# Dense products of a two-block transformer kernel: one float32 matmul each in place of three passes over split operands

## The chip, the cores and the metric

The kernel runs on one core of one Trainium2 chip, and the metric is the device time of one execution in microseconds. The engines are named as the profile names them: PE (TensorE's matmuls), PEld (its weight loads), DVE (VectorE), ACT (ScalarE), POOL (GpSimd), SP (the queue that issues most DMAs). TensorE's clock has two levels, 1.2 and 2.4 GHz; the profile gives the granted share of the higher one.

## The reference, cut to what matters

Two blocks follow each other, all in float32 (512 tokens, 1024 features). The first mixes tokens with a gated recurrence and a windowed attention, then sends the tokens through 16 experts. The second runs two layers over 16 + 512 tokens.

```python
# first block
h = rms_norm(x, norm1_g) * (1 + scale1) + shift1
proj = h @ w_in
mix = jnp.concatenate([y_mlstm, y_attn], axis=-1) @ w_out
x = x + gate1 * mix
x = x + gate2 * expert_choice_ffn(h2, ...)      # 16 experts of 64 tokens each
# second block, each of two layers (D = 1024, D_FF = 2816)
proj = h @ w_in
h = layer_norm(ALPHA * h + mix @ w_out, ln1_g, ln1_b)
y = (silu(h @ w1) * (h @ w3)) @ w2
h = layer_norm(ALPHA * h + y, ln2_g, ln2_b)
```

The products by `w_in`, `w_out`, `w1`, `w3` and `w2` outside the experts are the dense products of this document.

## The kernel before, in words

Features lie on partitions and tokens along the free dimension, so a dense product multiplies 128 x 128 weights (stationary) with 512, 264 or 256 tokens (moving) and sums over 8 feature tiles, or over the tiles of a part of the hidden features, in a bank of PSUM. The value projections have it the other way: 128 tokens stationary, 256 columns of weights moving.

Each operand is split: `split_w` (L416) makes `hi`, a copy by ACT in the type float32r, and `lo`, the rest, by DVE. `split_x` (L429, L430) does the same for products of the kernel's own, and the norms write `hi` and `lo` of the layer input (L1461, L1462). A product is then three matmuls on float32r operands: hi by hi, hi by lo, lo by hi (`mmh`, L1377 to L1379; `mmk`, L1389 to L1391, the same for several weight tiles; `values`, L717 to L719 and L1618 to L1620; `block`, L1985 to L1987).

The rest of PE's work has plain float32 operands: the experts (up L1171, down L1195, transposes L1182, gather L1154, scatter L1266), the sum of squares of the first norm (L570, eight matmuls), the attention and the recurrence, the rotation of the retention heads (L1588, one matmul for each of 4 tiles, 2 halves of the tokens and 2 layers).

The order of the work is written by a small planner, `_Stream`. Dense products stand in jobs. A job loads its weights some jobs ahead (`deep`), splits them some microseconds of announced cost ahead (`lead`), and its run yields the cost that it announces for each product, `3 * n / 2400.0` for n columns. Between the units of attention and recurrence, which go through generators, `S.step(STEP1)` or `S.step(STEP3 / 2)` emits so much announced cost of dense products. So the numbers set how many products stand between two units; the engines run in the order in which things were emitted.

Weights come in pieces of 1 MB through a ring, of 4 places in the first block and 2 in the second; a place is free when its weights are split. The input of the first dense product needs the results of `ada` jobs, which load two pieces each (L536) and multiply them at L555.

The upward products of the feed-forward, from the fourth tile of hidden features on, use Winograd's form of Strassen's product (`seven`): seven block products of 4 matmul products each, with sums of weights by DVE (L2004, L2005) and POOL (L2010, L2011), and sums of the layer input (`sums`) by POOL and DVE. `out` multiplies the two results and splits them into `H`; `down` multiplies `H` by `w2`, and `resid` (L1397, L1399) adds into `h`.

The layer input stands in `h` (for the residual) and split in `X`. During the mixer of the second block the values take the place of `h`, and when the last feature tile of the mixer is there, POOL adds `X`'s two parts back into `h` (L1911, 16 instructions a layer).

Of the kernel before, what the change touches and what calls it, by code (L numbers as in the profile page):

```python
# [12 lines left out]
F32R = mybir.dt.float32r  # L13
# [43 lines left out]
def _packed(v):  # L57
    """Features of the four retention heads in three tiles: a head of the first three each, and a third of the last."""
# [41 lines left out]
def _host(inp):  # L100
# [88 lines left out]
    # tables that depend on shapes alone  # L189
# [45 lines left out]
# ---------------------------------------------------------------- the program  # L235
# [9 lines left out]
class _Job:  # L245
# [11 lines left out]
    def prep(self, whole=True):  # L257
        """the rest of the preparation, or one step of it"""
# [12 lines left out]
class _Stream:  # L271
    """Dense products in the order of their emission. A job is prepared in two steps, the load of its weights
    (for the next `deep` jobs) and their split (`lead` us ahead). Its run yields the tensor engine's time in us, or None
    while it cannot go on; what has to wait for another engine goes to a tail."""
# [5 lines left out]
    def add(self, key, prep, run, cost=5.0, slow=0):  # L280
        """slow: the time between the steps of a preparation that goes along with the jobs before it"""
# [23 lines left out]
    def tail(self, g, job=None):  # L305
        """goes on with the steps of g, each after as much time as the one before it yields"""
# [16 lines left out]
    def _one(self):  # L323
        """emits one piece, returns its cost in us"""
# [30 lines left out]
    def until(self, key, flush=False):  # L355
        """goes on until the job is done; flush: its tails at once"""
# [13 lines left out]
    def weave(self, g, first, us):  # L370
        """the rest of the jobs, a step of g after each `us`"""
# [7 lines left out]
def _pipe(units):  # L379
    """the stages of the units, one behind the other"""  # L380
# [12 lines left out]
class _K:  # L393
    def __init__(self, nc, tc, A, at, out, dbg=None):
        self.nc, self.tc, self.A, self.at, self.out = nc, tc, A, at, out
        self.dbg = dbg or {}
        self.pin = False
# [905 lines left out]
    def second(self, ctx):  # L1303
# [17 lines left out]
        for c, g in self.cache.items():  # L1321
# [4 lines left out]
            if c == 0:  # L1326
                _drain(ln[0])
# [808 lines left out]
```

## Time and profile before

| what | before |
| --- | --- |
| device time, median of 3 runs | 2675.08 us (2674.12 to 2677.49) |
| profiled execution, span | 2671.3 us (the profile gives no other time for it) |
| PE, PEld busy | 2561.6, 1822.5 us |
| DVE, ACT, POOL busy | 1308.1, 849.1, 370.0 us |
| matmul records | 16400 |
| HBM read | 566.19 MB, 213 GB/s over the span |

The span is the time from the first to the last instruction of the profiled execution; its busy times are sums over the whole span, which has three parts: the mixer of the first block (to about 390 us), the experts (to about 1343), the second block. Records of matmuls overlap in time, since matmuls are pipelined.

### The profile page before, as it was taken

To read this page: it belongs to the slowest core of one execution; us is meant where nothing else is said; L and a number is where in the kernel's file an instruction comes from. 1 tells how busy PE (TensorE), PEld (TensorE's weight loads), DVE (VectorE), ACT (ScalarE), POOL (GpSimd) and SP (SyncE) were. 2 spreads that over 40 slices of the span, in tenths; PEclk is the share of its full clock that TensorE was granted. 3 is DMA by queue.
4 is the path that set the end of the run, shared out by engine and by line. 5 is a ranking of instruction groups with operands and counts; after the bars stand their busy time and mean duration, and the time that the engine had idled before them with its cause. 6 is when DMAs were issued, how large, how long until landed. Compare 5 with 4: busy or idle time off the path is not lost.

```text
span 2671.3 us, 39752 instructions
## 1 busy us (share of the span) xinstructions
PE 2561.6 (96%) x16400; PEld 1822.5 (68%) x16400; DVE 1308.1 (49%) x2483; ACT 849.1 (32%) x1601; POOL 370.0 (14%) x361
## 2 busy tenths in 40 slices
PE   7999989999999999999989998999999999899997
PEld 4777765333343433333478878999999888899997
DVE  5476750101010110101273568878876447978796
ACT  3455541000001010000133435434443434534344
POOL 0000010000000000000040125112223013511123
PEclk9999989999999999999989999999999999999999
DMA  7522459999999999999922112223332211232332
GB/s 306 192 93 96 166 196 384 420 402 419 419 419 420 420 420 419 420 419 419 379 86 90 45 57 81 93 95 102 105 109 94 88 46 56 95 103 88 102 108 73
DMA packets 104673, 570.93 MB, mean 214 GB/s; under 512 B 11598, under 2 KB 14926, under 8 KB 50988
## 3 DMA queue, kind: packets, MB, share of 16 engines
q1 hardware_dynamic: 101148, 561.45, 53.4%
q10 hardware_dynamic: 3344, 6.94, 0.8%
q8 instruction: 129, 2.11, 0.3%
q14 instruction: 52, 0.43, 0.0%
HBM read 566.19 MB, written 2.16 MB: 213 GB/s over the span
## 4 chain that ended last, share of the span: by engine, by line
PE 82%; DVE 12%; ACT 2%; DMA 2%; issue 1%; POOL 1%; DVEq 0%; ACTq 0%; POOLq 0%
PE gu L1171 18%; PE py L1195 8%; PE d L1377 6%; PE d L1379 6%; PE d L1378 6%; PE s L1985 5%; PE s L1987 5%; PE s L1986 5%; PE sc L1266 3%; PE sc L1154 3%; DVE wlo L416 2%; PE gt L1182 1%; DVE qlo L1462 1%; DMA ring<-in_w 1%; PE d L1618 1%; PE d L1619 1%
## 5 line engine op out<-in xcount | busy, mean ns | idle before, releaser
L416 DVE TENSOR_TENSOR wlo<-ring,whi 128x1024 fp32r<-128x1024 f32 (+2 forms) x253 | 305.3, 1210 | 126.2 <-ACT whi L416 125.7
L416 ACT ACTIVATE whi<-ring 128x1024 fp32r<-128x1024 f32 (+2 forms) x253 | 248.7, 989 | 354.3 <-PE d L1378 130.7
L1186 DVE TENSOR_TENSOR hd<-sg,gt 128x256 f32<-128x256 f32 x64 | 27.0, 422 | 640.9 <-ACT sg L1184 640.9
L1377 PE MATMUL d<-phi,whi 128*128 128x264 f32 (+1 forms) x888 | 254.4, 287 | 10.5 <-DVE h L1399 7.3
L1378 PE MATMUL d<-plo,whi 128*128 128x264 f32 (+1 forms) x888 | 251.0, 283 | 0.2
L1379 PE MATMUL d<-phi,wlo 128*128 128x264 f32 (+1 forms) x888 | 250.6, 282 | 0.0
L1171 PE MATMUL gu<-ew,xin 128*64 128x512 f32 x1008 | 247.8, 595 | 0.0
L1171 PE MATMUL gu<-ew,late 128*64 128x512 f32 x1024 | 247.4, 595 | 0.0
L1195 PE MATMUL py<-ew,hd 128*64 128x512 f32 x960 | 242.3, 599 | 0.0
L1173 ACT ACTIVATE gus<-gu 128x512 f32<-128x512 f32 x64 | 38.2, 597 | 486.5 <-PE gu L1171 486.5
L1171 PEld LDWEIGHTS gu<-ew,late 128*64 128x64 f32 x1024 | 75.2, 137 | 152.5 <-issue 148.2
L1377 PEld LDWEIGHTS d<-phi,whi 128*128 128x128 f32 x888 | 166.7, 188 | 17.8 <-issue 11.9
L1171 PEld LDWEIGHTS gu<-ew,xin 128*64 128x64 f32 x1008 | 81.7, 137 | 140.4 <-issue 128.6
L1378 PEld LDWEIGHTS d<-plo,whi 128*128 128x128 f32 x888 | 167.3, 188 | 1.4 <-DVE plo L430 0.6
L1379 PEld LDWEIGHTS d<-phi,wlo 128*128 128x128 f32 x888 | 167.2, 188 | 0.2 <-issue 0.2
L1377 PE MATMUL d<-qhi,whi 128*128 128x264 f32 (+1 forms) x496 | 151.9, 306 | 2.3 <-ACT qhi L1461 1.8
L1195 PEld LDWEIGHTS py<-ew,hd 128*64 128x64 f32 x960 | 69.9, 136 | 118.4 <-issue 112.4
L1378 PE MATMUL d<-qlo,whi 128*128 128x264 f32 (+1 forms) x496 | 146.8, 296 | 1.5 <-DVE qlo L1462 1.5
L1379 PE MATMUL d<-qhi,wlo 128*128 128x264 f32 (+1 forms) x496 | 146.8, 296 | 0.0
L1225 POOL TENSOR_TENSOR late<-h 128x528 f32<-128x528 f32 x1 | 1.3, 1315 | 946.7 <-ACT late L1223 946.7
L2010 POOL TENSOR_TENSOR ring<-ring 128x512 f32<-128x512 f32 x38 | 59.3, 1560 | 441.9 <-DVE glo L416 425.3
L1377 PEld LDWEIGHTS d<-qhi,whi 128*128 128x128 f32 x496 | 97.8, 197 | 14.1 <-issue 3.9
(492 smaller groups left out, 5950.4 us busy)
## 6 DMA issues: line engine op xcount, KB each, us to landing
ew<-in_wg SPq DMA_DIRECT2D x127, 1024.0 KB, 17.3
ew<-in_wu SPq DMA_DIRECT2D x127, 1024.0 KB, 16.1
ew<-in_wd SPq DMA_DIRECT2D x120, 1024.0 KB, 17.3
ring<-in_w SPq DMA_DIRECT2D x44, 1024.0 KB, 4.9
ring<-in_win SPq DMA_DIRECT2D x22, 1024.0 KB, 4.9
ring<-in_wada SPq DMA_DIRECT2D x21, 1024.0 KB, 6.2
ring<-in_wout SPq DMA_DIRECT2D x16, 1024.0 KB, 5.0
ring<-in_w SPq DMA_DIRECT2D x24, 640.0 KB, 3.9
```

The source lines that it names most:

```text
L416: both = (nc.scalar.activation(hi[:, :n], w, AF.Copy), nc.vector.tensor_sub(lo[:, :n], w, hi[:, :n].bitcast(F32)))
L1154: nc.tensor.matmul(ps[:, j], self.tok[:, t, 128 * k:128 * k + 128], oh[:, t].rearrange("p a b -> p (a b)"), start=(t == 0), stop=(t == 3))
L1171: nc.tensor.matmul(ps[64 * j:64 * j + 64], x, ws[k // 4][j][:, o], start=(k == 0), stop=(k == 7))
L1195: nc.tensor.matmul(py[64 * c:64 * c + 64], hd[:, j], wd[j // 2][:, o:o + 512], start=(n == 0 and j == 0), stop=(n == 3 and j == 3))
L1266: nc.tensor.matmul(ps, ys[e][s, 128 * (k % 4):128 * (k % 4) + 128], ogs[e][s], start=(i == 0), stop=(i == len(es) - 1))
L1377: nc.tensor.matmul(ps[:, :n], a, X[0][:p, k, r], start=(i == 0 and part != 1), stop=False)
L1378: nc.tensor.matmul(ps[:, :n], a, X[1][:p, k, r], start=False, stop=False)
L1379: nc.tensor.matmul(ps[:, :n], b, X[0][:p, k, r], start=False, stop=(i == len(ks) - 1 and part != 0))
L1985: nc.tensor.matmul(ps, a, x[0][:, k], start=(k == 0), stop=False)
L1986: nc.tensor.matmul(ps, a, x[1][:, k], start=False, stop=False)
L1987: nc.tensor.matmul(ps, b, x[0][:, k], start=False, stop=(k == 3))
L2010: nc.gpsimd.tensor_sub(a11, a21, a11)
```

## The change

Every dense product becomes one matmul on float32 operands, as they were loaded or computed. `split_w` and `split_x` go, with the tiles for the parts. The rings get 7 and 8 places, and a place is held until the last product with its weights. The layer input has a tile of its own (`X`, two buffers in the second block), the residual reads it from there, the norms write it once, and POOL's copies back go. The Winograd sums read `X` and write plain tiles. The announced costs and the steps all shrink to about two thirds. The comments of the file go as well.

```diff
-STEP1 = 4.0
-STEP3 = 2.4
+STEP1 = 2.7
+STEP3 = 1.6
...
-SUMGAP, PLAIN, HOLD, SLOW = 3.0, 3, 12.0, 2.1
+SUMGAP, PLAIN, HOLD, SLOW = 2.0, 3, 8.0, 2.0
...
-    def split_w(self, w, n, at=None):
-        hi, lo = [pool.tile([128, cols], F32R, name=tag + i, tag=tag + i, bufs=bufs) for i in ("hi", "lo")]
-        both = (nc.scalar.activation(hi[:, :n], w, AF.Copy), nc.vector.tensor_sub(lo[:, :n], w, hi[:, :n].bitcast(F32)))
...
-    def split_x(self, hi, lo, src):
-        nc.scalar.activation(hi, src, AF.Copy)
-        nc.vector.tensor_sub(lo, src, hi.bitcast(F32))
...
-        self.rp, self.ringcols, self.rbufs = pool("rp1"), 2048, 4
-        self.spl, self.nspl = pool("spl1"), 2
+        self.rp, self.ringcols, self.rbufs = pool("rp1"), 2048, 7
...
-                nc.scalar.activation(X[0][:, k], x, AF.Identity, scale=am[:, k:k + 1], bias=mod[:, k:k + 1])
-                nc.vector.tensor_scalar(x, x, am[:, k:k + 1], mod[:, k:k + 1], op0=OP.mult, op1=OP.add)
-                nc.vector.tensor_sub(X[1][:, k], x, X[0][:, k].bitcast(F32))
+                if k % 2:
+                    nc.scalar.activation(X[:, k], x, AF.Identity, scale=am[:, k:k + 1], bias=mod[:, k:k + 1])
+                else:
+                    nc.vector.tensor_scalar(X[:, k], x, am[:, k:k + 1], mod[:, k:k + 1], op0=OP.mult, op1=OP.add)
...
-                    ins = nc.tensor.matmul(ps, y_[0][s, o], og_[0][s], start=True, stop=False)
+                    ins = nc.tensor.matmul(ps, y[s, o], og[s], start=True, stop=True)
...
-                    nc.tensor.matmul(ps, y_[0][s, o], og_[1][s], start=False, stop=False)
-                    nc.tensor.matmul(ps, y_[1][s, o], og_[0][s], start=False, stop=True)
...
-        self.rp, self.ringcols, self.rbufs = pool("rp3"), 2048, 2
-        self.spl, self.nspl = pool("spl3"), 4
+        self.rp, self.ringcols, self.rbufs = pool("rp3"), 2048, 8
...
     def xt(self, n, k):
-        return tuple(self.xp.tile([128, k, L2], F32R, name=n + p, tag=n + p) for p in ("hi", "lo"))
+        return self.xp.tile([128, k, L2], F32, name=n, tag=n, bufs=2 if n == "q" else 1)
...
     def mmh(self, ps, r, ks, X, order=None, part=None, cut=None):
-            (hi, lo), j, k, p = ks[i if order is None else order[i]]
-            a, b = hi[:p, 128 * j:128 * j + 128], lo[:p, 128 * j:128 * j + 128]
-            nc.tensor.matmul(ps[:, :n], a, X[0][:p, k, r], start=(i == 0 and part != 1), stop=False)
-            nc.tensor.matmul(ps[:, :n], a, X[1][:p, k, r], start=False, stop=False)
-            nc.tensor.matmul(ps[:, :n], b, X[0][:p, k, r], start=False, stop=(i == len(ks) - 1 and part != 0))
-            yield 3 * n / 2400.0
+            w, j, k, p = ks[i if order is None else order[i]]
+            nc.tensor.matmul(ps[:, :n], w[:p, 128 * j:128 * j + 128], X[:p, k, r], start=(i == 0 and part != 1),
+                             stop=(i == len(ks) - 1 and part != 0))
+            yield 2 * n / 2400.0
...
-    def resid(self, m, r, ps, alpha):
+    def resid(self, m, r, ps, X=None):
...
-            self.nc.vector.scalar_tensor_tensor(x, x, alpha, ps, op0=OP.mult, op1=OP.add)
+            self.nc.vector.scalar_tensor_tensor(x, X[:, m, r], ALPHA, ps, op0=OP.mult, op1=OP.add)
...
-                hi, lo = X[0][:, k, r], X[1][:, k, r]
-                nc.scalar.activation(hi, t, AF.Identity, bias=bc)
-                nc.vector.scalar_tensor_tensor(lo, t, bc, hi.bitcast(F32), op0=OP.add, op1=OP.subtract)
-                if keep:
-                    nc.scalar.activation(x, t, AF.Identity, bias=bc)
+                nc.scalar.activation(X[:, k, r], t, AF.Identity, bias=bc)
...
-                for r in RO:
-                    for k in range(8):
-                        nc.gpsimd.tensor_add(self.h[:, k, r], X[0][:, k, r].bitcast(F32), X[1][:, k, r].bitcast(F32))
...
+                nc.gpsimd.tensor_sub(T[1][:, k], X[:, k, B_], X[:, k, A_])
+                nc.vector.tensor_sub(T[3][:, k], X[:, k + 4, B_], X[:, k, B_])
+                nc.gpsimd.tensor_sub(T[2][:, k], X[:, k + 4, B_], T[1][:, k])
+                nc.vector.tensor_sub(T[4][:, k], X[:, k + 4, A_], T[2][:, k])
...
-                nc.tensor.matmul(ps, a, x[0][:, k], start=(k == 0), stop=False)
-                nc.tensor.matmul(ps, a, x[1][:, k], start=False, stop=False)
-                nc.tensor.matmul(ps, b, x[0][:, k], start=False, stop=(k == 3))
-                yield 3 * nt / 2400.0
+                nc.tensor.matmul(ps, w[:, 128 * k:128 * k + 128], x[:, k], start=(k == 0), stop=(k == 3))
+                yield 2 * nt / 2400.0
...
-            nc.vector.tensor_mul(x, x, s[1][:, a:b])
-            self.split_x(H[0][:, place[f], r], H[1][:, place[f], r], x)
+            nc.vector.tensor_mul(H[:, place[f], r], x, s[1][:, a:b])
...
-                nc.gpsimd.tensor_sub(a11, a21, a11)
-                nc.gpsimd.tensor_sub(a12, a12, a11)
-                c = self.split_w(s3, 512, (fp, "c", 512, 2))
+                nc.gpsimd.tensor_sub(s2, a21, a11)
+                nc.gpsimd.tensor_sub(s4, a12, s2)
```

On PE, in the first Winograd tile of layer 0, the first block product ends and the second begins before with these rows (`qhi`, `qlo` the layer input, `t12` the sums of the input, `g` and `w` the split weights and their sums), one row for each pass:

```order
L1985 MATMUL s<-qhi,ghi 128x264
L1986 MATMUL s<-qlo,ghi 128x264
L1987 MATMUL s<-qhi,glo 128x264
L1985 MATMUL s<-t12hi,whi 128x264
L1986 MATMUL s<-t12lo,whi 128x264
L1987 MATMUL s<-t12hi,wlo 128x264
```

and now, from the second block product of that tile to its last (`t` the sums of the input, `ws` those of the weights, `ring` the weights as loaded):

```order
L1913 MATMUL s<-t_8350,ws 128x264 x4
L1913 MATMUL s<-q,ring 128x264 x4
L1913 MATMUL s<-t_8351,ws 128x264 x4
L1913 MATMUL s<-t_8349,ring 128x264 x4
L1913 MATMUL s<-t_8352,ring 128x264 x4
L1913 MATMUL s<-q,ws 128x264 x4
```

The 84 matmuls of a tile, three for a product, are 28, four in each row, and they read the ring itself.

On DVE, in the first norm of the second block (`var` its statistics, `nt` the normed input before the shift, `qlo` the low part of X, `wlo` that of weights), the second four feature tiles of the first half of the tokens stand before as

```order
L1459 SCALAR_TENSOR_TENSOR nt<-nt,cols,var 128x264 x4
L1462 SCALAR_TENSOR_TENSOR qlo<-nt,cols,qhi 128x264 x4
L1434 SCALAR_TENSOR_TENSOR var<-s,var 128x264
L416 TENSOR_TENSOR wlo<-ring,whi 128x1024 x2
L1435 TENSOR_SCALAR var<-var 128x264
L1583 TENSOR_SCALAR f<-d,cols 32x264
```

and the whole of that half now as

```order
L1216 SCALAR_TENSOR_TENSOR h<-sc,mod,h 128x512 x2
L1198 TENSOR_TENSOR late<-late,gus 128x528 x2
L1399 SCALAR_TENSOR_TENSOR var<-s,var 128x264
L1400 TENSOR_SCALAR var<-var 128x264
L1424 SCALAR_TENSOR_TENSOR nt<-nt,cols,var 128x264 x8
```

The eight multiplications of a half stand together, with no low part and no weight split among them.

## Rows read from the trace of the kernel before

**Rows 1.** Busy us of the engines by stretch (us from the start); records in brackets

```profile
core 0: us, PE busy (x) PEld busy (x) DVE busy (x) ACT busy (x) POOL busy (x), PEclk, DMA share, GB/s
0.00:390.00 390.00, 359.28 (x2205) 261.47 (x2206) 246.16 (x613) 192.36 (x403) 19.26 (x27) 0.97 0.46 175
390.00:1325.00 935.00, 920.50 (x4210) 363.06 (x4212) 96.80 (x163) 89.66 (x172) 0.00 (x0) 1.00 1.00 413
1343.00:1365.00 22.00, 16.25 (x58) 12.73 (x58) 19.87 (x30) 9.95 (x21) 13.36 (x15) 0.66 0.41 143
1700.00:2000.00 300.00, 297.30 (x2425) 295.43 (x2423) 238.57 (x365) 122.80 (x173) 62.51 (x46) 1.00 0.31 103
```

**Rows 2.** Line L1985, 1745 to 1756: count, ns min/median/max, first to last start

```profile
L1985 PE MATMUL s<-t12hi,whi x8: 280/284/287, 1746.0 to 1753.0; 128*128 128x264 f32 x8
L1985 PE MATMUL s<-qhi,whi x8: 280/284/287, 1747.5 to 1750.0; 128*128 128x264 f32 x8
L1985 PE MATMUL s<-qhi,ghi x8: 281/284/286, 1750.4 to 1754.4; 128*128 128x264 f32 x8
L1985 PE MATMUL s<-phi,chi x7: 281/283/291, 1744.9 to 1755.9; 128*128 128x264 f32 x7
```

**Rows 3.** Line L1377, 2448 to 2456: the same columns

```profile
L1377 PE MATMUL d<-phi,whi x24: 277/281/283, 2447.7 to 2455.9; 128*128 128x256 f32 x24
```

**Rows 4.** Timeline, PE, 512 columns: start us, duration us, line

```profile
48.87 0.39 PE L1377 MATMUL d<-xhi,whi 128*128 128x512 f32 x1
...
50.23 0.39 PE L1377 MATMUL d<-xhi,whi 128*128 128x512 f32 x1
```

**Rows 5.** Timeline, PE, around a rotation in layer 0 (L1588)

```profile
1390.10 1.94 PE L1588 MATMUL s<-rx,c_perm 128*128 128x264 f32 x8
1391.69 0.47 PE L1618 MATMUL d<-whi,qhi 128*128 128x256 f32 x1
1392.00 0.28 PE L1619 MATMUL d<-wlo,qhi 128*128 128x256 f32 x1
```

**Rows 6.** Groups by line and form: record count, busy us, mean ns of one

```profile
L1154 PE MATMUL sc<-oh,tok 128*128 128x128 f32 x512 | 71.4, 290 | 1.2 <-DVE oh L1146 1.2
...
L570 PE MATMUL o<-sq,ones 128*128 128x512 f32 x16 | 9.9, 787 | 7.2 <-ACT sq L569 7.2
```

**Rows 7.** Timeline, PE: gather with new weights each time, and heads (L796, L799)

```profile
1028.95 2.50 PE L1154 MATMUL sc<-oh,tok 128*128 128x128 f32 x20
...
136.42 1.12 PE L796 MATMUL s<-h,blk 128*128 128x512 f32 x2
137.38 1.02 PE L799 MATMUL s<-h,blk 128*128 128x512 f32 x2
```

**Rows 8.** Page, groups of instructions: busy us, mean ns, idle before

```profile
L416 DVE TENSOR_TENSOR wlo<-ring,whi 128x1024 fp32r<-128x1024 f32 (+2 forms) x253 | 305.3, 1210 | 126.2 <-ACT whi L416 125.7
L416 ACT ACTIVATE whi<-ring 128x1024 fp32r<-128x1024 f32 (+2 forms) x253 | 248.7, 989 | 354.3 <-PE d L1378 130.7
```

**Rows 9.** Timeline, DVE and POOL, first norm of the second block

```profile
1350.81 2.69 DVE L1462 SCALAR_TENSOR_TENSOR qlo<-nt,cols,qhi 128x264 fp32r<-128x264 f32 x4
...
1344.94 5.25 POOL L1458 TENSOR_TENSOR nt<-h,mu 128x264 f32<-128x264 f32 x6 [1.80 <-ACT mu L1432]
```

**Rows 10.** Waits of PE, 1343 to 2671: total us, times, longest us

```profile
PE d L1377 <- DVE h L1399: 7.3, 9, 1.4
PE d L1377 <- DVE h L1397: 5.6, 9, 2.1
...
PE s L1985 <- ACT fu L2022: 4.6, 2, 3.5
...
PE d L1389 <- DVE fs L2069: 2.0, 2, 1.2
```

**Rows 11.** Waits of SP's DMA queue, 0 to 60: total us, times, longest us

```profile
SPq L597 <- DVE wlo L416: 17.2, 2, 12.6
SPq L536 <- PE s L555: 12.9, 3, 6.2
```

More of the change, by code (lines that the diff above doesn't have):

```diff
@@ L706, in prep, with run @@
                 yield
-                return [self.split_w(w[:, 1024 * j:1024 * j + 1024], 1024) for j in range(2)]
-            def run(pcs):
+                return w
+            def run(w):
                 if "v" not in at:
@@ L948, in run @@
                 n = slice(rs[0].start, rs[-1].stop)
-                yield from self.mmh(ps, n, [(pc, k, k, 128) for k in range(8)], Y, order)
+                yield from self.mmh(ps, n, [(pc, k, k, 128) for k in range(8)], mix, order)
                 for r in rs:
@@ L1001, in first_mixer @@
         lb = scv[:, 64:80]
-        while active or (S.left() and Y is None):
+        while active or (S.left() and not out):
             for g in list(active):
@@ L1007, in first_mixer @@
             S.step(STEP1)
-            if not S.left() and Y is None:
-                Y = tuple(xp.tile([128, 8, 512], F32R, name="y" + p, tag="x" + p) for p in ("hi", "lo"))
+            if not S.left() and not out:
+                out = True
                 for c in range(4):
@@ L1200, in down_last @@
             s1, s2 = self.s12 = [hold()[1][:, L2 * i:L2 * i + L2] for i in range(2)]
-            parts = place(F32R)
-            og_, y_ = [[parts[:, 1024 * i + 512 * j:1024 * i + 512 * j + 512] for j in range(2)] for i in range(2)]
-            self.split_x(*og_, og)
+            y = place()[:, :512]
             def products(c, py, wd, js):
@@ L1421, with norm @@
     stats, seen = {}, {}
-    def norm(self, g, b, r, X, keep=True):
+    def norm(self, g, b, r, X):
         nc, h = self.nc, self.h
@@ L1471, in pair, with halves_of @@
         yield
-        return [self.split_w(w[:, n * j:n * j + n], n, at) for j in range(m)]
-    def halves_of(self, name, l, R, ws, n, run, cost, at={}, head=None):
+        return [w[:, n * j:n * j + n] for j in range(m)]
+    def halves_of(self, name, l, R, ws, n, run, cost, head=None):
         kept = {}
@@ L1490, in one @@
             job(c, r, lambda _: run(c, r, kept[c], js), cs, cost)
-        last = [c for c in range(4) if c in at or c > 1]
         if head:
@@ L1497, in halves_of, with wout @@
             one(c, R[0], (c,))
-        for c in (2, 3, 1, 0):
-            one(c, R[1], () if c in last else (c,))
-    def wout(self, l, R, M, order):
+        for c in range(4):
+            one(c, R[1], ())
+    def wout(self, l, R, M, order, X):
         def end(m, r, ps):
-            self.resid(m, r, ps, ALPHA)
+            self.resid(m, r, ps, X)
             self.stat(m, r)
@@ L1565, in run @@
                             between(m, r)
-            S.add(ms, prep, run, 5.4 * len(ms))
+            S.add(ms, prep, run, 3.6 * len(ms))
         qk = {}
@@ L1608, in prep, with run @@
                 yield
-                return [self.split_w(w[:, 1024 * j:1024 * j + 1024], 1024) for j in range(2)]
-            def run(pcs):
+                return w
+            def run(w):
                 for t in range(5):
@@ L1914, in step @@
                 out = True
-                self.wout(l, RO, M, order)
+                self.wout(l, RO, M, order, X)
                 S.prep()
-        while active or not out or not back:
+        while active or not out:
             for g in list(active):
@@ L2040, in run @@
                     self.lnexp()
-            S.add(("up", l, f), prep, run, 9.3, SLOW)
+            S.add(("up", l, f), prep, run, 6.2, SLOW)
         def up(fs):
```

176 lines of the change are left out of this document (61 added, 115 removed).

## The prediction, made before the change was run

> **What bounds the kernel now.** I read the busy time by stretch first, then the stream of matmuls in time, then the counts by form, and last the waits. [rows 1] shows three kinds of stretch. From 0 to 390 us the mixer of the first block keeps PE 359 us busy. From 390 to 1325 us the experts run with the DMA engines at a share of 1.00 and 413 GB/s: that stretch is paced by 1 MB transfers, and its products are float32 already. After it the second block is PE again: 297.3 of 300 us in the feed-forward of layer 0, at a granted clock of 1.00 and with DMA at 0.31. Only around 1343 to 1365, where the first norm of the second block stands, is PE at 16.3 of 22 with DVE at 19.9. So what an edit does to the dense products lands on the span in the first and third part and nowhere else.
>
> A busy PE says little of its pace, since the records overlap, so I take start to start. In [rows 2] 31 first passes of Winograd blocks with 264 tokens start within 11.0 us: 30 steps of 0.367 us, one step being a whole product of three passes. With 256 columns [rows 3] it is 23 steps in 8.2 us, 0.357. With 512 columns [rows 4] two products take 1.36 us, 0.68 each. Per pass that is 122, 119 and 227 ns: 0.42 ns for each further column, one column per cycle at 2.4 GHz, and 12 to 14 ns on top.
>
> **What a plain float32 matmul costs.** The trace of before holds the same operation on other operands. [rows 5] is the rotation of the queries, 128 x 128 weights and 264 tokens, amid the dense stream: eight records in 1.94 us, the last 0.386 long, so 0.222 us from start to start. The question that decides everything is how many such records one matmul leaves. [rows 6] answers it. The sum for the first norm is eight matmuls in the code (k = 0 to 7) and 16 records. The gather of the experts' inputs is 8 pairs x 2 halves x 16 = 256 matmuls and 512 records. A split pass is one record: the steps of [rows 2 to 4] count each product's first pass once. So a float32 product is two records, each of two cycles per column: four cycles per column, against three for three split passes. 264 columns cost 2 x 0.222 = 0.444 us, where the three passes cost 0.367; by columns (0.84 ns each) 0.431 for 256 against 0.357, and 0.861 for 512 against 0.68.
>
> The Trainium skill has a rule that points the other way: Perfetto Trace Analysis, Engine Utilization, puts TensorE's output rate at half for its low-high float32 mode, which read as a whole product would be 0.222 us; by that, the change would come out as in the first rival. The trace agrees with the half rate for a record, and shows two records.
>
> **The change part by part.** *Dense products.* By the loops there are 152 products of 512 columns and 160 of 256 in the first block, 1588 of 264 and 1348 of 256 in the second (48 of these with 16 weight columns), and 8 small ones at the last expert. The price differences: 1588 x 0.077 = 122.3 us, 1508 x 0.074 = 111.6, 152 x 0.181 = 27.5, together **261 us more** of PE, 39 in the first block and 222 in the second. Nearly all of it is on the path, since PE has 1 us in 100 to spare in the dense stretches [rows 1]. What could make it dearer is that each record has new weights, which [rows 5] (one matrix throughout) doesn't show. The gather does change them with each matmul: 20 records in 2.50 us, the last 0.29 long [rows 7], 0.116 each where 128 columns at 0.84 ns are 0.107. So 0 to 9 ns for each of 6,496 records, 0 to 58 us. I take 0, because 264 columns give a weight load twice the time to hide that 128 give it, and keep 58 for the upper end.
>
> *Splits.* 253 weight pairs cost DVE 305 us and ACT 249 [rows 8], and the parts of X come on top. All of that goes. It is beside PE's work, so it gives back only where PE waited. I credit four places. (a) The first norm of the second block: DVE alternates four multiplications with four low parts, and PE, at a mean granted share of 0.66, so in part at 1.2 GHz, waits for them in pieces [rows 1]. Four low parts take 2.69 us [rows 9], the sixteen of both halves 11, and they go from between the multiplications. The eight subtractions of a half on POOL then set the pace (six in 5.25 us [rows 9]). I take 8 us, between 0 and, with a weight split or two, 14. (b) Waits for the residual sums (h) that free the two result banks, 7.3 + 5.6 us [rows 10]: at the output projection they stand behind POOL's 32 copies of X into h, which go, and otherwise behind splits on DVE. I take 7 of 12.9. (c) Waits for the first Winograd sums and for the hidden features of the first tiles, 4.6 + 2.0 us [rows 10]: 4 of 6.6. (d) The start: the queue of the loads waits 17.2 us for a split and 12.9 for PE before it may refill one of four ring places [rows 11]; with seven, the second half of the modulation comes sooner. PE sits idle only part of that. I take 6, between 0 and 12. Together **25 us back**, 0 to 46, and by estimate 10 more if the granted clock falls less often than in [rows 1].
>
> *Costed at nothing.* The step sizes and job costs all shrink by the same third as the cost that a product announces (STEP1 4.0 to 2.7 for 0.64 to 0.427), so as many products stand between two attention units as before. Eight ring places hold weights until PE is done with them; transfers take 0.31 of DMA in the dense stretch [rows 1], and if a place came free late PE would wait for at most one 1 MB load, about 5 us, per stage. The residual reads X in place of h with the same operation. The experts' DMA stretch moves as a block, since its first 17 places are filled while the first block ends in either kernel. At the last expert 8 products of 64 rows grow by some 0.2 us each, and 2 us of waits for the split of y go.
>
> **Sum.** Span 2671.3 + 261 - 25 = 2907.3. The profiled execution is given by its span alone; the median of the three runs stands 3.8 us above it, so 2911.
>
> **The rivals.** *Faster: one record is the whole price.* If the second record came only with matmuls of the kinds seen so far, or ran under the next one, products would cost 0.222, 0.216 and 0.431 us: 1588 x 0.145 + 1508 x 0.141 + 152 x 0.249 = 481 us less, and with 25 back about 2169. The cost that a product announces in the new code (2 n / 2400 for 3 n / 2400) would fit this, but it is no measurement. Against it: in [rows 5] the next dense pass starts early but needs 0.31 us to its successor, where 0.12 is usual, so the second record's columns are paid. It decides at one point: a product below 0.367 us is a gain. A neighbour of it is that weight loads are the bound: PEld is 295.4 of 300 us busy [rows 1], and two loads replace three. The Trainium skill (Perfetto Trace Analysis, Identifying the Most-Contended Engine) takes the busy share of weight loads as the better sign of a full TensorE. By two thirds of the three-pass price the dense work would shrink by 3248 x 0.12 = 390 us, to about 2260 with the same 25. Against it stands that the pass grows with its columns at one per cycle [rows 2 to 4], which a load of 128 columns wouldn't make it do. Together 0.05.
>
> *Slower still: weight loads in the open.* The first record of a float32 product after another kind costs 0.10 us more (1.12 against 1.02 us for a pair [rows 7]). If each product paid that once, 3248 x 0.10 = 325 us come on top: 3236. The gather pays at most 9 ns, so 0.03.
>
> *Hidden after all.* If the freed DVE and ACT had been PE's pace throughout, 261 would be given back; PE's waits after 1343 us add up to too little for that. 0.01 for a time within 0.2% of before (5 us, about what a measurement of this kernel can tell from no change).
>
> **Numbers.** The forecast, four cycles per column for three with a little given back, has 0.91; its own bounds are 2880 (56 back) and 2989 (58 dearer, 5 back). The upper end needs the gather's worst price everywhere, so I stop at 2955, and go down to 2878; that leaves the range about 0.82. Faster 0.05, same 0.01, slower 0.94.
>
> **What would show it.** Dense lines with two records per product, 0.22 us apart in the feed-forward stretches at clock 1.00, and about 6,500 dense records where there were 9,768; PE still above 98% busy there; the two feed-forward stretches of 300 us grown to about 363; the experts' stretch still about 935 us; DVE below 950 us in all; no wait for a split. Wrong if a 264-column product starts 0.22 us after the one before it, or if PE shows gaps before dense products.

## The result: 7.3% slower, and 40 us faster than forecast

Four runs of the changed kernel have a median of **2870.77 us** (2870.70 to 2872.78), four of the kernel before on the same chip 2674.60 (2672.97 to 2677.49): a ratio of 1.073, with a 95% interval of 1.0715 to 1.0745. The prediction had the direction and put 2911 with a lower end of 2878. The profiled execution is this one; the first lines of the page are span, then busy time, share and instructions of each engine:

```profile
span 2869.1 us, 32042 instructions
...
PE 2788.1 (97%) x13144; PEld 1815.4 (63%) x13144; DVE 850.1 (30%) x1963; ACT 496.3 (17%) x1129; POOL 287.6 (10%) x329
```

DVE lost 458 us and ACT 353, PE gained 227. Below are the stretches that answer to [rows 1], each at the same place of the program: first block, experts, first norm of the second block, feed-forward of layer 0.

```profile
0.00:411.00 411.00, 385.51 (x1893) 228.89 (x1894) 197.30 (x558) 155.50 (x358) 14.77 (x27) 0.99 0.44 165
411.00:1346.00 935.00, 918.96 (x4162) 362.10 (x4164) 94.42 (x159) 88.41 (x170) 0.00 (x0) 1.00 0.99 408
1367.00:1389.00 22.00, 16.02 (x51) 11.11 (x52) 15.27 (x24) 11.46 (x26) 15.14 (x19) 0.82 0.77 297
1720.00:2020.00 300.00, 300.00 (x1350) 256.30 (x1349) 98.48 (x196) 14.94 (x30) 40.25 (x28) 1.00 0.25 84
```

In that stretch of the feed-forward PE has no idle time left, and the granted clock around the first norm is 0.82 where it was 0.66. The price of a product answers to [rows 2] and [rows 4]; the timeline of PE in the changed kernel, Winograd products of 264 columns and then products of 512, with start, duration, line and count:

```profile
1800.57 1.94 PE L1913 MATMUL s<-t,ws 128*128 128x264 f32 x8
1802.35 1.94 PE L1913 MATMUL s<-q,ring 128*128 128x264 f32 x8
1804.13 1.94 PE L1913 MATMUL s<-t,ws 128*128 128x264 f32 x8
...
47.49 4.88 PE L1345 MATMUL d<-x,ring 128*128 128x512 f32 x11
```

Eight records every 1.78 us are 0.2225 each, two per matmul: 0.445 us for a product, as forecast from the rotation [rows 5]. Of PE's waits after the first norm, which answer to [rows 10], this is left (total, times, longest, in us):

```profile
PE d L1355 <- DVE p L1990: 8.5, 2, 4.4
PE s L1548 <- ACT rx L1545: 6.5, 2, 3.5
...
PE d L1345 <- ACT q L1425: 2.0, 3, 1.7
...
PE s L1394 <- POOL s L1380: 1.4, 1, 1.4
...
PE d L1345 <- DVE h L1362: 0.2, 1, 0.2
```

The waits for the residual sums h are 0.2 us where they were 12.9. The 8.5 us on L1355, waits for the multiplication that makes the hidden features of the first tiles, were 2.0 before. The 1.4 us for GpSimd's sums of the norms' statistics were 5.2, a line that [rows 10] leaves out:

```profile
PE s L1429 <- POOL s L1415: 5.2, 3, 1.9
```

### The profile page after: what moved, and what is told of

Read it like the earlier page. It is cut to its first block, busy times and chain, and to the rows that moved or that the text cites. A ratio compares the mean times of both kernels' runs of the same rounds, so it can differ in the third digit from the quotient of the medians.

```text
span 2869.1 us, 32042 instructions
## 1 busy us (share of the span) xinstructions
PE 2788.1 (97%) x13144; PEld 1815.4 (63%) x13144; DVE 850.1 (30%) x1963; ACT 496.3 (17%) x1129; POOL 287.6 (10%) x329
## 4 chain that ended last, share of the span: by engine, by line
PE 93%; DVE 4%; ACT 1%; DMA 1%; issue 0%; POOL 0%; SPq 0%; DVEq 0%; ACTq 0%; POOLq 0%
PE d L1345 27%; PE gu L1147 17%; PE s L1913 16%; PE py L1171 8%; PE d L1576 4%; PE sc L1238 3%; PE sc L1130 2%; PE gt L1158 1%; PE s L1345 1%; PE s L1660 1%; DVE nt L1424 1%; PE d L695 1%; PE d L1355 1%; PE o L1668 1%; PE s L1730 1%; PE s L809 1%
## 5 line engine op out<-in xcount | busy, mean ns | idle before, releaser
L1345 PE MATMUL d<-p,ring 128*128 128x264 f32 (+1 forms) x1888 | 420.1, 383 | 1.6 <-ACT p L1762 1.4
L1345 PEld LDWEIGHTS d<-p,ring 128*128 128x128 f32 x1888 | 357.6, 190 | 58.7 <-ACT p L1762 1.9
L1345 PE MATMUL d<-q,ring 128*128 128x264 f32 (+1 forms) x992 | 239.0, 394 | 2.0 <-ACT q L1425 2.0
L1345 PEld LDWEIGHTS d<-q,ring 128*128 128x128 f32 x992 | 186.1, 192 | 44.3 <-ACT q L1425 4.6
L1913 PE MATMUL s<-q,ring 128*128 128x264 f32 (+1 forms) x608 | 145.7, 383 | 0.0
L1913 PE MATMUL s<-t,ws 128*128 128x264 f32 (+1 forms) x608 | 145.7, 383 | 0.0
L1913 PE MATMUL s<-t,ring 128*128 128x264 f32 (+1 forms) x608 | 139.5, 383 | 0.0
L1913 PEld LDWEIGHTS s<-q,ring 128*128 128x128 f32 x608 | 115.6, 190 | 17.7
L1913 PEld LDWEIGHTS s<-t,ring 128*128 128x128 f32 x608 | 115.6, 190 | 17.7
L1345 PE MATMUL d<-x,ring 128*128 128x512 f32 x272 | 122.3, 595 | 1.6 <-DVE x L764 1.6
L1919 ACT ACTIVATE late<-late 128x528 f32<-128x528 f32 (+3 forms) x40 | 24.6, 615 | 417.6 <-DVE late L1958 410.3
## 6 DMA issues: line engine op xcount, KB each, us to landing
ew<-in_wd SPq DMA_DIRECT2D x120, 1024.0 KB, 16.5
```

What stands on the lines that cost most here:

```text
L1345: nc.tensor.matmul(ps[:, :n], w[:p, 128 * j:128 * j + 128], X[:p, k, r], start=(i == 0 and part != 1), stop=(i == len(ks) - 1 and part != 0))
L1913: nc.tensor.matmul(ps, w[:, 128 * k:128 * k + 128], x[:, k], start=(k == 0), stop=(k == 3))
```

## Where the time went, stage by stage

I cut both traces at the same places (first expert matmul; first matmul of each layer norm) and take from each stage its dense records times their price, the median from one start to the next of the same form: 122, 119 and 227 ns before (264, 256, 512 columns), 223, 216 and 429 after. What is left is the time that is no dense product, here called the **rest** (us). One ns in a price moves a sum by 3 us; comparisons of kernels at equal price don't depend on it.

| stage | before | after | float32 on split parts | dead splits on VectorE | before, no low weights |
|---|---|---|---|---|---|
| first block | 236.4 | 218.5 | 223.7 | 227.6 | 228.5 |
| experts | 946.2 | 949.6 | 946.3 | 949.0 | 947.1 |
| mixer, layers 0 / 1 | 108.6 / 95.7 | 91.9 / 86.5 | 101.9 / 95.1 | 95.7 / 88.0 | 101.1 / 91.0 |
| output projection, second half | 7.3 / 7.0 | 0.8 / 0.8 | 3.8 / 3.8 | 8.8 / 9.2 | 1.6 / 1.8 |
| feed-forward | 10.4 / 13.6 | 6.0 / 8.0 | 12.8 / 11.6 | 16.5 / 17.3 | 2.3 / 5.7 |
| its last second half | 5.7 / 4.1 | 0.8 / 2.9 | 4.5 / 3.4 | 3.6 / 2.9 | 3.7 / 3.8 |
| tail | 13.3 | 13.3 | 14.1 | 13.3 | 13.6 |
| all | 1448.2 | 1379.1 | 1421.1 | 1431.8 | 1400.3 |

The dense records cost 1223 us before and 1490 after, 267 more (261 forecast). The rest fell by **69 us where the prediction put 25**. That difference of 44 us is the error; the price, 6 us above the forecast, takes some of it off again.

## The experiments

Two theories of the 69 us. **A, the pace:** a slower PE leaves every other engine more time, so waits vanish by themselves. **B, the structure:** what went with the change (splits of weights, splits of X, copies, small ring) had delayed PE. Medians stand beside those of the kernel before on the same chip, 2672.0 to 2676.2.

### Slower passes with all the splits

```
                 nc.tensor.matmul(ps, b, x[0][:, k], start=False, stop=False)
+                nc.tensor.matmul(ps, b, x[1][:, k], start=False, stop=(k == 3))
```

> The kernel before with a fourth float32r pass (low part by low part) in each dense product; splits, copies and orders stay. 1588 x 0.122 + 1508 x 0.119 + 152 x 0.227 = 408 us more for TensorE. Theory A (a slower TensorE by itself hides waits: all other engines have the same work and more time for it): the part of the time that is no dense pass falls as it did with the change, by about 68 us, so 2675 + 408 - 68 = about 3015. Theory B (the waits went because the splits, copies and orders went): nothing of that happens, about 3080.

3029.2 us, ratio 1.1327 (1.1309 to 1.1344). The rest fell by 48 (1448.2 to 1400.1). So a slower pace can take waits away by itself. But this pace, 0.488 us per product, is slower than that of the change.

### The kernel before without the low parts of the weights

```
-        both = (nc.scalar.activation(hi[:, :n], w, AF.Copy), nc.vector.tensor_sub(lo[:, :n], w, ...))
+        lo = hi
+        both = (nc.scalar.activation(hi[:, :n], w, AF.Copy),)
```

> The kernel before, but the low part of each weight is not computed (253 subtractions, 305 us of VectorE) and the third pass of each product reads the high part again. It leaves out the low parts of the weights from the result; the count and the size of the passes are the same. Theory B with the weights' splits as its main part: the time falls by 20 to 60 us, to 2615 to 2655. Theory A, or theory B with another part (order of the second halves, parts of X, copies of X, rings): within 10 us of 2675.

2626.1 us, ratio 0.9823 (0.9807 to 0.9840): 48 us faster at an unchanged pace, in the middle of what B expected. (The subtractions taken away are 333 and 415 us, not 253 and 305: the Winograd groups have 80 more under other names.) A alone can't do this. The table's last column shows it in every stage but the experts and the tail.

### Dead splits beside the changed kernel

Both halves of each weight split go to tiles that nobody reads; then each engine's half alone.

```
+    def split_w(self, w, n):
+        hi, lo = [self.spl.tile([128, 1024], F32, ...) for i in ("hi", "lo")]
+        nc.scalar.activation(hi[:, :n], w, AF.Copy)
+        nc.vector.tensor_sub(lo[:, :n], w, hi[:, :n])
+        return w
-                return cache[c][:, 1024 * j:1024 * j + 1024]
+                return self.split_w(cache[c][:, 1024 * j:1024 * j + 1024], 1024)
```

> The changed kernel with the weights' splits put back on ScalarE and VectorE as dead work: both parts go to tiles that nobody reads, TensorE still takes the unsplit weights. Room for the tiles comes from the rings: 6 places in place of 7 in the first block, 7 in place of 8 in the second. Theory A: 2871, up to 10 more, since a slow TensorE leaves VectorE the time. Theory B with the weights' splits as its main part: 2871 + 20 to 60.

2920.0 us, ratio 1.0917 (1.0901 to 1.0933): 49 us over the changed kernel, though PE reads none of it.

> The changed kernel with VectorE's half of the dead splits alone (one subtraction per weight split into a tile nobody reads; ScalarE does none), with 6 and 7 ring places as in the run with both halves, which gave back 48 us. If the place in VectorE's own order is what PE waits for (sums of results standing behind subtractions), nearly all returns: 2905 to 2920. If it is the pair of ScalarE and VectorE (one waiting for the other), less than half: 2871 to 2890.

2924.0 us, ratio 1.0930 (1.0915 to 1.0945): **53 us** come back with VectorE's half alone. Its two groups in this kernel, busy time and mean:

```profile
L411 DVE TENSOR_TENSOR wlo<-ring 128x1024 f32<-128x1024 f32 (+2 forms) x245 | 290.8, 1187 | 77.0 <-DMA ring<-in_wout 38.3 <-DMA ring<-in_winv 22.7 <-DMA ring<-in_win 11.8
L411 DVE TENSOR_TENSOR wlo<-ws 128x512 f32<-128x512 f32 x114 | 113.9, 999 | 3.9
```

> The changed kernel with ScalarE's half of the dead splits alone (one copy per weight split into a tile nobody reads), 6 and 7 ring places again. If VectorE's order is the cause: 2871 to 2880. If ScalarE's, or the smaller rings: 2890 to 2920.

2873.6 us, ratio 1.0741 (1.0726 to 1.0755), 3 us over the changed kernel with 313 us of ScalarE's copies put back and the same smaller rings. So it is VectorE's own order, neither ScalarE nor the rings. What it doesn't settle: the dead splits stand near, not at, the places of the old ones (none is repeated for the second halves, and those of the first Winograd groups fall beside the output projections), so the 53 needn't be the share of the old ones. By the table it isn't: 39 of it come in the second halves and the feed-forward parts, where the change had given back 28.8, but only 9.1 of the first block's 17.9 and 5.3 of the mixers' 25.9.

### Parts of the change undone one at a time

```
-        self.rp, self.ringcols, self.rbufs = pool("rp1"), 2048, 7
+        self.rp, self.ringcols, self.rbufs = pool("rp1"), 2048, 4
```

> The changed kernel with 4 ring places for loads in the first block in place of 7. The first block lost 18 us beside its dense products with the change. If the deeper ring is the reason, the time rises by 6 to 15 us (2877 to 2886) and the first block by as much. If the splits that went are the reason, the time stays at 2871 within 4.

2870.75 us, ratio 1.0732 (1.0717 to 1.0746): nothing. The deeper ring of the first block is worth nothing.

```
+                        nc.gpsimd.tensor_copy(self.h[:, k, r], X[:, k, r])
-            self.nc.vector.scalar_tensor_tensor(x, X[:, m, r], ALPHA, ps, op0=OP.mult, op1=OP.add)
+            self.nc.vector.scalar_tensor_tensor(x, x, ALPHA, ps, op0=OP.mult, op1=OP.add)
```

> The changed kernel with the layer input again in h: 32 copies of X into h on GpSimd at the end of the mixers, 32 more activations in the norms of the feed-forward part, and residuals that read h. If the input's own tile is a main part of what came back, the time rises by 5 to 15 us, in the mixers and at the output projections; if the splits are all of it, within 4 us of 2871.

2873.0 us, ratio 1.0737 (1.0722 to 1.0752): 2 us, inside the spread of its runs (2867 to 2876). Beside the changed kernel the copies cost nothing that can be seen.

```
                 nc.scalar.activation(X[:, k, r], t, AF.Identity, bias=bc)
+                nc.vector.scalar_tensor_tensor(x, t, bc, X[:, k, r], op0=OP.add, op1=OP.subtract)
```

> The changed kernel with the low part of the layer input computed in the norms as before (one VectorE instruction per feature tile and half), into the dead place of h where nobody reads it. If the low parts in the norms are a main part of the 69 us, the time rises by 8 to 20 us, most of it at the start of the mixer of layer 0. If the weights' splits are the main part there too, within 4 us of 2871.

2872.7 us, ratio 1.0739 (1.0725 to 1.0754): 2 us. But this total hides two opposite effects. The rest of three second halves (both output projections and the end of layer 0's feed-forward) rises from 0.8 each to 5.1, 3.8 and 4.0 us, so there the low parts do cost, 10.5 us. The rest of the feed-forward parts falls from 6.0 and 8.0 to 0.2 and 1.4, because a wait of the changed kernel goes, the 8.5 us of the result section. Its rows in the changed kernel (VectorE does Winograd sums of the input, then L1990, which PE waits for):

```profile
1694.89 0.42 DVE L1905 TENSOR_TENSOR t<-q,t 128x264 f32<-128x264 f32 x1
1695.24 0.42 DVE L1903 TENSOR_TENSOR t<-q 128x264 f32<-128x264 f32 x1
1695.58 0.42 DVE L1990 TENSOR_TENSOR p<-fs,d 128x264 f32<-128x264 f32 x1
1696.05 1.25 PE L1355 MATMUL d<-q,ring 128*128 128x264 f32 x2 [4.11 <-DVE p L1990]
```

and in this run, where the first of these multiplications stands ahead of the Winograd sums, with the wait that is left:

```profile
1697.52 0.42 DVE L1991 TENSOR_TENSOR p<-fs,d 128x264 f32<-128x264 f32 x1
...
1702.00 0.42 DVE L1904 TENSOR_TENSOR t<-q 128x264 f32<-128x264 f32 x1
...
PE d L1355 <- DVE p L1991: 0.6, 1, 0.6
```

So 8.5 us of waits become 0.6. The 64 low parts are no main part of the total, but not because they cost nothing. And an order that puts the multiplication first should save the changed kernel some 8 us, an estimate that no run here tests.

### Unsplit operands at the old pace

```
+def product(nc, ps, w, x, start, stop):
+    w, x = [a.bitcast(BF16)[:, 1::2] for a in (w, x)]
...
+    nc.tensor.matmul(ps, w, x, start=start, stop=False)
+    nc.tensor.matmul(ps, z, x, start=False, stop=False)
+    return nc.tensor.matmul(ps, z, x, start=False, stop=stop)
```

> The changed kernel with the price of before: each dense product is three one-cycle passes on the unsplit operands read as bfloat16 (the upper halves of the float32 words), the first on the weights and two on a tile of zeros, so that the product stands at bfloat16 accuracy and its low bits are left out. No splits, and the changed kernel's rings, orders and buffers. If such a pass takes the 0.122, 0.119 and 0.227 us of the float32r passes, theory B (the waits went with the splits, copies and orders) gives 2871 - 261 = about 2610; theory A (they went because TensorE is slower) gives the old waits back, about 2675.

2574.4 us, ratio 0.9623 (0.9608 to 0.9637). Its passes are a little cheaper than the split ones (117, 113 and 226 ns), so its dense records sum to 1172 where 1223 was assumed; the rest is 1401, 47 below the kernel before. B gives most of it at a fast pace too. By stage, its first block (218.9) and its mixers (92.4 / 86.2) stand where the changed kernel's do; its feed-forward parts (11.5 / 14.0) and the second halves of its output projections (4.9 / 5.1) don't, so there the gain needs the slower pace too.

### The pace of the change with the splits of before

A fourth pass on 5/8 of the columns was to give that pace:

```
+                nc.tensor.matmul(ps[:, :nt * 5 // 8 // 4 * 4], b, x[1][:, k, :nt * 5 // 8 // 4 * 4], start=False, stop=False)
                 nc.tensor.matmul(ps, b, x[0][:, k], start=False, stop=(k == 3))
```

> The kernel before, its splits, copies and orders unchanged, with a short fourth pass in each dense product (low part by low part on the first 5/8 of the columns: 164 of 264, 160 of 256, 320 of 512), so that a product costs about what it costs after the change: by 0.42 ns per column and 12 on top, 0.080, 0.079 and 0.146 us more, 1588 x 0.080 + 1508 x 0.079 + 152 x 0.146 = 268 us. The result gets a part of the low-by-low terms more than before. If the price alone gave the 69 us back, 2674 + 268 - 69 = 2873. If the price alone gave nothing, 2942. Dead splits on VectorE beside the changed kernel gave back 53 of the 69, which leaves 16 to the price: 2926. A straight line to the run with four whole passes (48 back for 408) gives 31: 2911.

3044.9 us, ratio 1.1398 (1.1382 to 1.1415), above all four values and above four whole passes. The price was not the one wanted: a product of 264 columns takes 122 + 122 + 76 + 158 = 478 ns (the section on the hardware has its rows), and the dense records sum to 1591. Even so it speaks against A: the rest is 1452, not below the 1448 of before, although the pace is close to that of four whole passes, which took 48 away. PE's waits for h in the second block are 27.4 us here and 4.9 there. In the second half of the output projection of layer 0, VectorE's 41 instructions take 28.0 us here and 25.8 there (this run, then four whole passes; the columns of [rows 1]):

```profile
1689.30:1725.40 36.10, 31.89 (x258) 31.04 (x256) 28.04 (x41) 18.50 (x36) 17.60 (x15) 1.00 0.25 89
1696.80:1730.50 33.70, 31.94 (x258) 31.38 (x257) 25.75 (x41) 18.52 (x36) 15.26 (x15) 1.00 0.27 95
```

So the price alone doesn't say how much a slower pace gives back; what makes these two runs differ stays open. To compare at the changed kernel's own price, that price itself was used:

```
+def one(nc, ps, hi, lo, k, start, stop):
+    w, x = [y.bitcast(F32) for y in (lo if k % 2 else hi)]
+    nc.tensor.matmul(ps, w, x, start=start, stop=stop)
```

> The kernel before with all its splits, copies, orders, buffers and step sizes, but one float32 matmul per dense product in place of the three passes, on the high parts for even k and on the low parts for odd k, so that TensorE still waits for both. It leaves two of the three partial products out. The price per product is then that of the changed kernel, 0.444, 0.431 and 0.861 us, 261 us more than before. If the price by itself gives back all 69 us: 2674 + 261 - 69 = 2866. If it gives back nothing: 2935. If the dead splits on VectorE measured the part of the splits (53), the price is left with 16: about 2919. A straight line to the run with four whole passes gives 31: 2904.

2912.9 us, ratio 1.0882 (1.0866 to 1.0898). Its dense records have the medians of the changed kernel (223, 216, 429 ns), so the two compare without any price: **42 us** lie between them, which the structure is worth at this pace. The rest is 1421.1, 27 below the kernel before: that is what the pace alone gives back. 27 + 42 = 69. In the other order, structure first, it is 47 (the run with unsplit operands at the old pace) and then 22. So the theories aren't rivals but overlap, and their shares depend on which comes first: what one has freed the other can't free again.

### Two tries for a faster kernel

```
+        low = nc.gpsimd if tag == "c" or (at is None and self.turn % 2 and not self.pin) else nc.vector
```

> The kernel before with a part of the low parts of the weights computed on GpSimd in place of VectorE: every second one of the splits of loaded pairs (1024 columns, an estimated 3.1 us each from the 1.56 us of 512 columns) and the 512-column split of each Winograd group. All the parts are computed, only on another engine. If VectorE's load is what PE waited for, the time falls by 10 to 25 us, to 2650 to 2665. If a split's own latency or its buffers are it, the time stays or rises, since GpSimd is 2.6 times slower.

2730.8 us, ratio 1.0210 (1.0196 to 1.0224): slower, by 57 us. VectorE's remaining work became dearer. The first row is of the kernel before, the others are of this one; the mean in ns stands behind the busy time:

```profile
L416 DVE TENSOR_TENSOR wlo<-ring,whi 128x1024 fp32r<-128x1024 f32 x189 | 247.8, 1315 | 110.1 <-ACT whi L416 109.5
...
L419 DVE TENSOR_TENSOR wlo<-ring,whi 128x1024 fp32r<-128x1024 f32 x133 | 193.2, 1453 | 104.2 <-ACT whi L419 103.4 <-DMA ew<-in_wg 0.5
...
L1419 DVE TENSOR_TENSOR s<-s,sq 128x264 f32<-128x264 f32 (+1 forms) x56 | 50.6, 903 | 17.4 <-ACT sq L1417 17.2
```

```
-        return [self.split_w(w[:, n * j:n * j + n], n, at) for j in range(m)]
+        for j in range(m):
+            out.append(self.split_w(w[:, n * j:n * j + n], n, at))
+            yield
```

> The kernel before, with the splits of a loaded pair of weight tiles spread over the products ahead of them (one split per 2.0 us of announced work) in place of two in a row, in the mixers' products, both output projections and the down products of the second block. The same work. If PE waits because a sum of results stands behind two splits in a row, the time falls by 5 to 20 us, to 2655 to 2670, at the output projections and in the mixers. If it waits for the split itself, it stays or rises.

2677.2 us, ratio 1.0009 (1.0000 to 1.0018): no change, so two splits in a row are not what PE waited for. The runs point to no version that computes all parts and beats the kernel before.

## The mechanism in one stage

The second half of the output projection of layer 0 shows it best. The same stretch of five kernels, in the columns of [rows 1] (length, then PE, PEld, DVE, ACT, POOL, clock, DMA). Before:

```profile
1609.30:1639.60 30.30, 25.07 (x195) 23.98 (x193) 28.56 (x41) 18.62 (x36) 18.97 (x15) 1.00 0.30 105
```

After:

```profile
1651.00:1679.90 28.90, 28.90 (x131) 24.68 (x131) 13.85 (x27) 8.56 (x20) 14.18 (x17) 1.00 0.37 118
```

Float32 on the split parts:

```profile
1662.80:1694.70 31.90, 29.66 (x132) 24.24 (x130) 27.91 (x41) 18.43 (x36) 18.29 (x15) 1.00 0.30 100
```

Dead splits on VectorE:

```profile
1663.20:1700.10 36.90, 29.64 (x131) 24.34 (x129) 29.25 (x40) 9.00 (x20) 19.02 (x19) 0.98 0.30 104
```

The kernel before without low parts of the weights:

```profile
1594.80:1619.40 24.60, 24.23 (x196) 23.92 (x195) 15.32 (x33) 18.99 (x36) 12.15 (x15) 1.00 0.37 129
```

**VectorE sets the pace here, not PE**: 28.56 of 30.3 us before. The change adds 5 us of matmuls to this stage and makes it shorter. Without the low parts of the weights PE sets the pace, 24.23 of 24.6. With the dead splits neither engine is full (29.6 and 29.3 of 36.9), so VectorE's load alone doesn't explain that run; the order of its work must count too. The timeline of before shows the order of work on VectorE (start, duration, line):

```profile
1618.28 0.41 DVE L1399 SCALAR_TENSOR_TENSOR h<-h,d 128x264 f32<-128x264 f32 x1
1618.62 1.21 DVE L416 TENSOR_TENSOR wlo<-ring,whi 128x1024 fp32r<-128x1024 f32 x1
1619.75 1.90 DVE L1462 SCALAR_TENSOR_TENSOR qlo<-nt,cols,qhi 128x264 fp32r<-128x264 f32 x2
1621.57 0.42 DVE L1416 TENSOR_TENSOR s<-s,sq 128x264 f32<-128x264 f32 x1
1621.92 0.48 DVE L1459 SCALAR_TENSOR_TENSOR nt<-nt,cols,var 128x264 f32<-128x264 f32 x1
1622.32 0.41 DVE L1399 SCALAR_TENSOR_TENSOR h<-h,d 128x264 f32<-128x264 f32 x1
```

From one residual sum h to the next it has 4.04 us of work without a gap, of which the weight split is 1.21, while a product of eight times 0.367 us is done in 2.9. And PE in the same stretch, the passes around two product boundaries:

```profile
1618.41 0.28 PE L1379 MATMUL d<-phi,wlo 128*128 128x264 f32 x1
1618.84 0.36 PE L1377 MATMUL d<-phi,whi 128*128 128x264 f32 x1
...
1621.71 0.28 PE L1379 MATMUL d<-phi,wlo 128*128 128x264 f32 x1
1622.88 0.36 PE L1377 MATMUL d<-phi,whi 128*128 128x264 f32 x1 [0.89 <-DVE h L1399]
```

These rows also show why the table of waits misled me. The second boundary takes 1.17 us where 0.12 is usual, a loss of 1.05; the table counts 0.89, because the modelled end of a pass (0.28 long, where the next start is usual after 0.12) hides the first 0.16 us of each gap. The first takes 0.43, a loss of 0.31, and the table counts nothing. PE's waits in this stage, from the table:

```profile
PE d L1377 <- DVE h L1399: 3.2, 3, 1.4
PE s L1429 <- POOL s L1415: 1.9, 1, 1.9
```

With the gaps too short for the table PE is idle for 5.2 us, 3.3 at the residual sums and 1.9 at the end, where the norm waits for GpSimd's sum of the statistics. Its loss is about 6.5 (7.3 against 0.8); eight gaps with 0.16 us hidden make up the difference of 1.3.

## Where the prediction was right, and where it was wrong

- **The price: right.** Two records per product, 0.2225 us each, 6,496 dense records, weight loads hidden as chosen (0 of 0 to 58). The feed-forward of layer 0 grew from 348.2 to 417.6 us, by 1.20 where 300 to 363 meant 1.21. DVE is at 850 us, below 950.
- **The faster rivals: fallen.** A product takes 0.445, not 0.222. The weight loads' share of the feed-forward stretch fell from 295.4 to 256.3 of 300 us while that work became dearer.
- **(a), the first norm: the size right, the cause in part.** 8 put. Up to the 40th dense product of the second block the rest fell from 21.0 to 13.9, 7.1 us; float32 on the split parts has 17.5 there, so the pace alone gave half of it, which the prediction didn't count.
- **(b), the residual sums: mis-sized.** "I take 7 of 12.9." The table's waits for h fell by 12.7, and the four second halves gave back 18.8 (6.5 + 6.2 + 4.9 + 1.2). Of that, 14.0 was idle time, 3.8 of it the wait for GpSimd's statistics, which the prediction doesn't name; the other 4.8 are in no table of waits, so 12.9 was no bound. The copies on POOL that the prediction names give nothing when put back (2 us, within the spread).
- **(c), first Winograd sums and hidden features: mis-sized, and not by these waits.** 4 put, 10.0 measured in the two feed-forward parts. But of the two waits named only the first went (4.6 to none); the second rose from 2.0 to 8.5.
- **(d), the start: the wrong cause and too small.** 6 put, for the ring. Four places do as well as seven. The first block lost 17.9; up to its 96th dense product 12.3 (63.9 to 51.6), of which the pace alone gives 6.9 (57.0).
- **Left out:** the two mixers after the first norm, 18.8 us (9.6 + 9.2). VectorE isn't full there (119.8 of the 232 us of layer 0 before). Of the 25.9 us that the mixers lost with the first norm, the low parts of the weights give 12.2 when they alone go, and the changed structure gives nearly all at the old pace; which of its other parts do it stays open. Against it, the experts' stage lost 3.4. 7.1 + 18.8 + 10.0 + 17.9 + 18.8 - 3.4 = 69.2.
- **The clock: nothing in the sum, 10 us in the upper bound.** The time at the lower of the two levels, as the records grant it, fell from 95 to 57 us over the span. In it start 181 dense passes before and 33 dense records after, at medians of 220 in place of 122 ns (264 columns, split) and 440 in place of 223 (float32). That is about 20 us more than at the upper level before and 7 after, so by estimate 13 of the 69 came with the clock. Float32 on the split parts has 9 to 10, so most of this came with the pace.

So the step that failed is "Together 25 us back, 0 to 46". It sized what comes back by some of the waits that the table names. PE's idle time, span less busy, fell by only 28.7 us (109.7 to 81.0) while the rest fell by 69: what a gap hides at its start and what the lower clock costs are part of the difference, and stand in no wait. It put nothing for PE's own slower pace, though that pace was the forecast's main term. With 27 for the pace and 42 for the structure in its place, the sum is 2671.3 + 267 - 69 = 2869; as these are measured, that closes the account and tests nothing.

## What to carry to other kernels

When an edit slows the bounding engine, ask which waits its slowness itself removes; three slower paces gave 48, 27 and nothing here, so test it and don't credit a fixed share. Measure slack stage by stage as length less records times their start-to-start price, not as idle time. A stage of 30 us can be bound by an engine that the span shows at half load, so read each engine's busy share in windows around layer norms and short products. To learn what work on a side engine costs, put it back as dead work that nobody reads: two such runs told VectorE from ScalarE here. Read such a run by stage as well, since a total of 2 us hid 10.5 us lost and 12.4 gained.

## What the runs showed of the hardware beyond the expected

A **short pass makes the next one longer**. Timeline of PE in the run with the short fourth pass:

```profile
2301.94 0.32 PE L1381 MATMUL d<-qhi,wlo 128*128 128x264 f32 x1
2302.10 0.28 PE L1378 MATMUL d<-qhi,whi 128*128 128x264 f32 x1
2302.22 0.28 PE L1379 MATMUL d<-qlo,whi 128*128 128x264 f32 x1
2302.34 0.24 PE L1380 MATMUL d<-qlo,wlo 128*128 128x164 f32 x1
2302.42 0.32 PE L1381 MATMUL d<-qhi,wlo 128*128 128x264 f32 x1
2302.58 0.28 PE L1378 MATMUL d<-qhi,whi 128*128 128x264 f32 x1
```

The 164 columns take 0.08 us to the next start, and the full pass behind them 0.16 instead of 0.12 (medians 76 and 158 ns). Together 234, or 117 per pass, although only 428 of 528 columns are streamed. That fits a load of new weights of about 117 ns (an estimate) that a pass hides only if it is as long itself. A short pass of 320 columns, 144 ns, is longer, and the pass behind it hardly grows: 232 ns where 227 is usual. The Trainium skill (TensorE: Matmul & The Clock Gate, LDWEIGHTS) gives a load the time of its columns at 1.2 per ns, 107 ns for 128; the trace agrees within 10 ns. If so, the split passes of 256 columns, at 119 ns, stood just above the price of their loads: nearer to the second faster rival than the prediction thought.

**Work on GpSimd slows VectorE, while both run.** With 56 splits of 1024 columns, 24 of 640, 8 of 896 and 38 of 512 on GpSimd, VectorE's own splits of 1024 columns took 1453 ns where they took 1315, and its sums of squares 903 where they took 714. The trace of before shows the same thing one instruction at a time:

```profile
1620.41 0.95 POOL L1458 TENSOR_TENSOR nt<-h,mu 128x264 f32<-128x264 f32 x1
1621.57 0.42 DVE L1416 TENSOR_TENSOR s<-s,sq 128x264 f32<-128x264 f32 x1
1624.45 1.83 POOL L1458 TENSOR_TENSOR nt<-h,mu 128x264 f32<-128x264 f32 x2
1624.70 0.98 DVE L1416 TENSOR_TENSOR s<-s,sq 128x264 f32<-128x264 f32 x1
```

The sum of squares takes 0.42 us with GpSimd idle and 0.98 beside a GpSimd instruction. Of 189 splits of 1024 columns before, the 107 with no GpSimd instruction beside them take 1227 ns at most; the 82 others take 1442 in the mean and up to 2312. With splits on GpSimd the 57 that overlap take 1768 in the mean. The residual sums of 264 columns (L1397, L1399), which read one operand from PSUM, don't grow: 423 ns alone and 418 beside GpSimd. The Trainium skill (SBUF — State Buffer, SBUF: two separate sides) has a port pair that VectorE and GpSimd hold in turn, one blocking the other; these rows agree with it.
